# Code-row loads moved behind the last first-layer weight load, GpSimd's memsets ahead of its one-hots, and GELU's square between ScalarE's one-hots

## The chip, the core and the metric

The kernel runs on one core of one Trainium2 chip. The metric is device time in microseconds: the median over several runs, lower is better. The engines are TensorE (PE, its weight loads PEld), VectorE (DVE), ScalarE (ACT), GpSimd (POOL) and SyncE (SP), whose queue issues most DMA transfers.

## What is computed

One layer of a hybrid decoder trunk for 256 tokens of width 2048: a norm, one input projection, a pooling mixer beside a gated recurrence, an output projection, and then a product-key retrieval (PEER) over 128 x 128 single-neuron experts with 8 heads and the top 16 each. The change touches the retrieval only:

```python
q = (zc @ peer_wq).reshape(PEER_CHUNK, PEER_HEADS, 2, PEER_HALF)
s1 = einsum('chd,hkd->chk', q[:, :, 0], k1); s2 = einsum('chd,hkd->chk', q[:, :, 1], k2)
v1, i1 = top_k(s1, 16); v2, i2 = top_k(s2, 16)
...
top_s, top_pos = top_k(cand, 16)
expert = take_along_axis(cand_idx, top_pos)            # i1 * 128 + i2
gate = softmax(top_s)
act = gelu(einsum('chkd,cd->chk', take(peer_u, expert), zc))
w = gate * act
return einsum('chk,chkd->cd', w, take(peer_v, expert))
```

So each token has 128 chosen experts (8 heads x 16), each named by a pair (i1, i2) of numbers below 128.

## The kernel before

**The stages.** The front part (mixers and projections) comes first and is not touched. The *first expert layer* multiplies all 16384 rows of the first 1536 columns of `peer_u` with all tokens: 192 weight units (64 pairs of keys, GU = 3 units each) of 128 x 1024 numbers. Each unit is loaded by SP (line 99, `raw<-in_u_dram`), split into a rounded part `hi` by ACT (line 109) and a rest `lo` by DVE (line 110), and used in 24 matmuls (lines 359 to 361). ACT carries finished scores to `sw` (line 862). The other 512 columns are gathered row by row on POOL (line 684) and dotted on DVE (line 694) into `sg`. `sw` then holds every expert's score, from which the *slot stage* takes the chosen ones: 32 slots of 8 tokens. The *second expert layer* (lines 1095 to 1097) streams `peer_v` against the weights that the slot stage has written back to `sw`.

**A slot.** `extract_mm(n)` (lines 982 to 993) makes 8 small bf16 matmuls (986) of bits of i2, kept in a code buffer, with a table of codes, which push every wrong i2 far down, and adds to them the product of a one-hot of i1 (`ohts`, four buffers) with the scores (991). `extract_pick(n)` (996, DVE) takes the maximum. After every fourth slot GELU is computed for 32 tokens: `gelu_1` (DVE, 1004 and 1005), `gelu_1s` (ACT, a Square, 1009), `gelu_2` (DVE, 1013 and 1014), `gelu_2s` (ACT, a Tanh, 1018), `gelu_3` (DVE, 1022), which writes the weights `wt`. With LAG = 6 slots between, `form_mm(f)` (1063) multiplies a one-hot of i1 by a weighted one-hot of i2, and `form_out` (1067, ACT) writes the result to `sw`. `one(n)` makes the one-hot of i1: on ACT, eight Abs (1033) and a Relu (1036), or on DVE, one comparison (1029); the strings `O1_BY` and, for the last six slots, `O1_LAST` say which ("a" or "d"). `two(n)` makes the weighted one-hot of i2: on DVE a comparison (1049) and a product (1058), and on POOL (1045) the tokens that `by_pool` gives it, which in the last six slots are two of eight.

**What sets the order.** Each engine and each DMA queue runs its instructions in the order of the program, and this order is written out by hand: there is no scheduler here. In the first layer `u` counts the units; at unit `nu - 11` the work for the slot stage begins. `load_ib(k)` (869, SP) brings the i1 of slot k to all partitions (`ibt`, two buffers, 256 KB each), `onehot_t(k)` (882 on POOL or DVE, 879 and 880 on ACT) makes the transposed one-hots from them, `prepare_codes()` clears the table tile `asw` on POOL (894), copies the code table into it on ACT (897), and calls `code_tile(k)`, which clears a code buffer on POOL (906) and then loads four times 8 KB into it from SP (909). The three code buffers lie in the tiles `i1f`, `i2f` and `sg`. `Stream.ahead` issues the weight loads: each waits on SP for a free buffer, that is, for an earlier unit's `lo`.

Of the kernel before, what the change touches and what calls it, by code (L numbers as in the profile page):

```python
# [10 lines left out]
F32 = mybir.dt.float32  # L11
# [9 lines left out]
T = 256  # L21
# [20 lines left out]
SB = 32  # L42
TB = 32
LAG = 6
O1_BY, O1_LAST = "aaaad", "add"
O1_EARLY, O2_EARLY = 3, 5
O2_POOL, O2_POOL_LAST = (1, 0), 2
OHT_BY = "ppappdpapd"
NCB, V_LOAD, V_SPLIT = 3, 9, (14, 18)
# [109 lines left out]
def kernel(ctx: ExitStack, tc: tile.TileContext, x, cols, front, gates_w, keys, u1, u2, v1, v2,  # L159
                      g2row, gfrow, code, out):  # L160
    nc = tc.nc
# [3 lines left out]
    cst = ctx.enter_context(tc.tile_pool(name="cst", bufs=1))  # L165
# [5 lines left out]
    n_v = len(units) - v1.shape[0]  # L171
# [22 lines left out]
    zg = cst.tile([128, 2, D2], F32, name="zg", tag="zg")  # L194
# [18 lines left out]
    def bank(tag, bufs):  # L213
        return psA.tile([128, 512], F32, name=tag, bufs=bufs)
# [3 lines left out]
    st = Stream(nc, wst, xpool, units, SWITCH)  # L218
# [138 lines left out]
    def three(o, ah, al, bh, bl, first, last):  # L357

        nc.tensor.matmul(o, ah, bh, start=first, stop=False)  # L359
        nc.tensor.matmul(o, ah, bl, start=False, stop=False)  # L360
        nc.tensor.matmul(o, al, bh, start=False, stop=last)  # L361
# [211 lines left out]
    for c in range(4):  # L573
        acc = [bank("mm", 4) for _ in range(2)]
        for kp in range(8):
            wh, wl = st.take()
            for k2 in range(2):
                k = kp * 2 + k2
# [276 lines left out]
    def flush_evac():  # L855
        while evac:
            pi, ev = evac.popleft()
            if (pi // SB + 1) * SB * T > top[0]:
                while steps.queue or steps.plan:
                    steps.tick(10 ** 9)  # L860
                assert issued[0] - len(flying) >= GFIRST
            nc.scalar.activation(swb[:, pi // SB, :, pi % SB], ev[:, :T], AF.Copy)

    NP = T // 8
# [24 lines left out]
    ctab, code_buf = [], []  # L889

    def prepare_codes():

        tabs = asw[:, 3, :].bitcast(BF).rearrange("p (g k) -> p g k", g=4)
        nc.gpsimd.memset(tabs, 0.0)
        for g in range(4):
            gs = slice(32 * g, 32 * g + NCODE)
            nc.scalar.activation(tabs[gs, g, :], wtok[gs, 0, :], AF.Copy)
            ctab.append(tabs[:, g, :])
        code_buf.extend(t.rearrange("p a b c -> p (a b c)").bitcast(BF) for t in (i1f, i2f))
        code_buf.append(sg.rearrange("p a b -> p (a b)").bitcast(BF))  # L900
        code_tile(0)
        code_tile(1)

    def code_tile(k):
        if k < NCB:
            nc.gpsimd.memset(code_buf[k], 0.0)
        for q in range(4 * k, min(4 * k + 4, T // 4)):
            g = q % 4
            nc.sync.dma_start(code_buf[k % NCB][32 * g:32 * g + NCODE],
                              code_dram[:, q * 4:q * 4 + 4, :].rearrange("k t s -> k (t s)"))  # L910

    nu = 64 * GU
    done0 = done[0]
    for pr in range(64):
        acc = [bank("mm", 4) for _ in range(2)]
        for kg in range(GU):
            wh, wl = st.take()
            for j in range(2):
                for k in range(4):
                    kk = kg * 4 + k  # L920
                    o = (j * 4 + k) * 128
                    three(acc[j][:, :T], wh[:, o:o + 128], wl[:, o:o + 128], z2h[kk], z2l[kk], kk == 0, kk == KU - 1)
            flush_evac()
            if pr == 0 and kg == 0:
                for tag in ("zbhi", "zblo"):
                    g = zbpool.tile([128, 2, D2], F32, name="gat" + tag, tag=tag)
                    gbuf2 += [g[:, 0, :], g[:, 1, :]]
                g = gp.tile([128, 2, D2], F32, name="gatp", tag="gat")
                gbuf2 += [g[:, 0, :], g[:, 1, :]]
            u = pr * GU + kg  # L930
            side(min(256, done0 - (done0 - 256) * (u + 1) // (nu - DOT_END)) - done[0])
            if u == nu - DOT_END + 1:
                assert done[0] == 256
                ibt = zbpool.tile([128, 2, 8, 128], BF, name="ibt", tag="zbhi")
                ohts.append(zbpool.tile([128, 8, 128], F32, name="ohta", tag="zblo"))
                ohts.append(gp.tile([128, 8, 128], F32, name="ohtb", tag="gat"))
                for k in range(2):
                    load_ib(k)
                for k in range(2):
                    onehot_t(k)  # L940
                asw = cst.tile([128, 4, T], F32, name="asw", tag="zg")
                prepare_codes()
            if u == nu - 8:
                p = bank("tp", 2)
                for i in range(2):
                    nc.tensor.transpose(p[:, i * 128:(i + 1) * 128], sg[:, i, :], ident)
                nc.scalar.activation(asw[:, 1, :], p[:, :T], AF.Copy)
                code_tile(2)
            if u == nu - 3:
                for k in (2, 3):  # L950
                    load_ib(k)
            if u == nu - 1:
                early2 = [by8(v[1]) for v in list(st.raw_free)[:O1_EARLY]]
                for k in range(O1_EARLY):
                    nc.vector.tensor_tensor(early2[k], *rows(i2t, k), op=OP.is_equal)
        for j in range(2):
            evac.append((2 * pr + j, acc[j]))
# [49 lines left out]
    def gelu_1s(b):  # L1007
        a, g, c = gel[b]
        nc.scalar.activation(g, a, AF.Square, scale=math.sqrt(GELU_C))

    def gelu_2(b):
        a, g, c = gel[b]
        nc.vector.scalar_tensor_tensor(g, g, 1.0, a, op0=OP.add, op1=OP.mult)
        nc.vector.tensor_tensor(c, a, gtt[:, b * TB:(b + 1) * TB], op=OP.mult)

    def gelu_2s(b):
        g = gel[b][1]
        nc.scalar.activation(g, g, AF.Tanh, scale=GELU_S)
# [5 lines left out]
    def one(n, mid=lambda: None):  # L1024

        o = o1(n)
        if (O1_LAST[n % len(O1_LAST)] if n >= NP - LAG else O1_BY[n % len(O1_BY)]) == "d" and n >= O1_EARLY:
            mid()
            nc.vector.tensor_tensor(o, *rows(i1t, n), op=OP.is_equal)  # L1029
            return  # L1030
        for j in range(8):
            t = n * 8 + j
            nc.scalar.activation(o[:, j, :], iota, AF.Abs, scale=-1.0, bias=i1t[:, t:t + 1])  # L1033
            if j == 3:
                mid()
        nc.scalar.activation(o, o1(n, True), AF.Relu, scale=-1.0, bias=1.0)  # L1036
# [11 lines left out]
        k = 8 - by_pool(n)  # L1048
        nc.vector.tensor_tensor(o2(n)[:, :k], *rows(i2t, n, k), op=OP.is_equal)  # L1049

    def two(n, mid):

        if n >= O2_EARLY:
            two_a(n)
        mid()
        k = 8 - by_pool(n)
        o = o2(n)[:, :k]
        nc.vector.tensor_tensor(o, o, rows(wt, n, k)[1], op=OP.mult)  # L1058
# [7 lines left out]
    def form_out(n):  # L1066
        nc.scalar.activation(swb[:, :, n * 8:n * 8 + 8, :], fob.pop(n).rearrange("p t (b i) -> p b t i", i=SB), AF.Copy)  # L1067
# [36 lines left out]
    for n in range(NP + LAG + 1):  # L1104
        b, f = n // G - 1, n - LAG
        gelu = n % G == 0 and 0 <= b < T // TB
        if gelu:
            gelu_1(b)
        if n < NP:
            extract_mm(n)  # L1110
        if 0 <= f + 1 < NP:
            two_pool(f + 1)
        if n < NP:
            onehot_t(n + 4)
            load_ib(n + 6)
        if 0 <= f < NP:
            form_mm(f)
        if 0 <= f - 1 < NP:
            form_out(f - 1)
        if gelu:  # L1120
            gelu_1s(b)
        g2, g2s = ((lambda: gelu_2(b)), (lambda: gelu_2s(b))) if gelu else [lambda: None] * 2
        if 0 <= f + 1 < NP:
            two(f + 1, g2)
            if f + 1 >= O1_EARLY:
                one(f + 1, g2s)
            else:
                g2s()
        else:
            g2()  # L1130
            g2s()
        if n < NP:
            extract_pick(n)
        if O1_EARLY <= n + 2 < O2_EARLY:
            two_a(n + 2)
        if n < O1_EARLY:
            one(n)
        if n == V_LOAD:
            st.limit = len(units)
            while st.load():  # L1140
                pass
        if n in V_SPLIT:
            st.give_back()
            st.split()
            st.load()
        if gelu:
            gelu_3(b)
        if n == NP + 1:
            acc_bank()
            acc_bank()  # L1150
            w_split(0, slice(0, 128))
        if n in (NP + 3, NP + 4):
            c = n - NP - 3
            v_mm(0, c, 0, *st.hl[st.used + c][1:])
        if n % G == 1 and (b + 1) * TB % 128 == 0 and 0 <= b < T // TB:
            w_token((b + 1) * TB // 128 - 1)
# [50 lines left out]
    for pr in range(62):  # L1207
# [7 lines left out]
        if 16 <= pr < 48 and pr % 2 == 0:  # L1215
            n = (pr - 16) // 2
# [126 lines left out]
```

## Time and profile before

| | |
|---|---|
| median of 3 runs | 1650.94 us (1648.98 to 1651.82) |
| profiled execution: its own time | 1647.0 us |
| its span, first to last instruction | 1645.1 us |
| mean granted TensorE clock | 0.986 |
| busy share PE / PEld / DVE / ACT / POOL | 96% / 89% / 82% / 53% / 57% |
| HBM traffic over the span | 253 GB/s |

A row of the timeline gives start and length of an instruction (or of several alike in sequence), and in brackets how long its engine had waited just before and what ended that wait. Line numbers are those of the kernel before. PE is busy for 96% of the span, so that a stretch in which it is not, or in which its clock is granted at half, is what to look for.

### The profile page before, as it was taken

The page shows a single profiled execution, that of the slowest core. Times are in us where ns is not written, and L with a number is a line of the kernel's source. Part 1 is how long each engine was busy: PE and PEld are TensorE (multiplying, and loading weights), DVE is VectorE, ACT ScalarE, POOL GpSimd, SP SyncE. Part 2 cuts the span into 40 slices and gives each one's busy share as a digit, 9 for nine tenths or more (in the row PEclk, how much of TensorE's full clock was granted, in tenths as well). Part 3 has the DMA queues.
Part 4 walks back from the last instruction along what each step waited for, and adds up shares of the span by engine and source line. Part 5 has one row for each costly group of instructions (what it writes and reads, how often), then busy time and mean ns, then how long its engine had stood idle before and what let it go on. Part 6 is the DMA issues. An engine that isn't in the chain of part 4 may idle for free. (4 is left out here: it accounts for less than half of the span.)

```text
span 1645.1 us, 28958 instructions
## 1 busy us (share of the span) xinstructions
PE 1579.3 (96%) x10734; PEld 1461.1 (89%) x10734; DVE 1351.0 (82%) x2300; ACT 876.2 (53%) x1212; POOL 935.7 (57%) x753
## 2 busy tenths in 40 slices
PE   8899999999999999999999789989999999999996
PEld 8899888999999999999999789978888888888885
DVE  7799755899999997777777269888988898988897
ACT  6676544444444445445444358865555555555554
POOL 2476201267567766555554148856767876666662
PEclk9999999999999999999999899999999999999998
DMA  7455666578888888999998423209999999999992
GB/s 252 143 169 180 206 210 192 169 238 277 305 291 279 284 283 294 322 310 314 304 311 288 144 68 118 71 10 328 323 326 337 332 351 357 361 337 330 349 323 91
DMA packets 124974, 418.61 MB, mean 254 GB/s; under 512 B 18128, under 2 KB 20720, under 8 KB 124704
## 3 DMA queue, kind: packets, MB, share of 16 engines
q1 hardware_dynamic: 82528, 278.70, 51.4%
q0 software_dynamic: 42304, 138.06, 23.7%
q8 instruction: 84, 1.38, 0.3%
q14 instruction: 58, 0.48, 0.1%
HBM read 411.90 MB, written 4.78 MB: 253 GB/s over the span
## 5 line engine op out<-in xcount | busy, mean ns | idle before, releaser
L109 ACT ACTIVATE hi<-raw 128x1024 fp32r<-128x1024 f32 x390 | 413.0, 1059 | 479.2 <-PE mm L360 329.6
L110 DVE TENSOR_TENSOR lo<-raw,hi 128x1024 fp32r<-128x1024 f32 x390 | 500.4, 1284 | 199.1 <-ACT hi L109 196.9
L361 PE MATMUL mm<-zahi,lo 128*128 128x256 f32 x2016 | 576.0, 286 | 13.9 <-DVE lo L110 13.7
L359 PE MATMUL mm<-zahi,hi 128*128 128x256 f32 x2016 | 576.0, 286 | 10.3 <-ACT hi L109 10.3
L360 PE MATMUL mm<-zalo,hi 128*128 128x256 f32 x2016 | 573.8, 285 | 0.0
L1174 POOL DMA_INDIRECT gatv<-in_v_dram,e x256 | 335.9, 1312 | 170.2 <-DVE accg L1184 109.2
L361 PEld LDWEIGHTS mm<-zahi,lo 128*128 128x128 f32 x2016 | 389.6, 193 | 17.8 <-DVE lo L110 17.6
L359 PEld LDWEIGHTS mm<-zahi,hi 128*128 128x128 f32 x2016 | 389.9, 193 | 10.6 <-ACT hi L109 10.5
L360 PEld LDWEIGHTS mm<-zalo,hi 128*128 128x128 f32 x2016 | 390.0, 193 | 0.0
L1095 PE MATMUL acc<-hi,wht 128*128 128x512 f32 x512 | 200.8, 392 | 5.0 <-DVE sw L1230 3.2
L1097 PE MATMUL acc<-hi,wlt 128*128 128x512 f32 x512 | 200.5, 392 | 0.0
L1096 PE MATMUL acc<-lo,wht 128*128 128x512 f32 x512 | 200.4, 391 | 0.0
L1184 DVE SCALAR_TENSOR_TENSOR accg<-gatv,wtok,accg 128x512 f32<-128x512 f32 x252 | 184.2, 751 | 5.8 <-DMA gatv<-in_v_dram,e 5.6
L684 POOL DMA_INDIRECT sw<-in_u_dram,e x96 | 116.2, 1210 | 83.8 <-DVE sw L694 39.6
L1095 PEld LDWEIGHTS acc<-hi,wht 128*128 128x128 f32 x512 | 96.5, 189 | 25.9 <-DVE sw L1230 2.8
L1097 PEld LDWEIGHTS acc<-hi,wlt 128*128 128x128 f32 x512 | 96.7, 189 | 20.5 <-DVE wlt L1086 0.4
L1096 PEld LDWEIGHTS acc<-lo,wht 128*128 128x128 f32 x512 | 96.7, 189 | 20.3 <-DVE lo L110 0.4
L1095 PE MATMUL acc<-more,wht 128*128 128x512 f32 x256 | 100.1, 391 | 0.0
L1096 PE MATMUL acc<-more,wht 128*128 128x512 f32 x256 | 99.9, 390 | 0.0
L1097 PE MATMUL acc<-more,wlt 128*128 128x512 f32 x256 | 99.9, 390 | 0.0
L684 POOL DMA_INDIRECT gatzblo<-in_u_dram,e x54 | 61.6, 1140 | 47.7 <-DVE gatzblo L694 36.1
L684 POOL DMA_INDIRECT gatzbhi<-in_u_dram,e x54 | 60.9, 1129 | 45.3 <-DVE gatzbhi L694 29.1
(304 smaller groups left out, 2626.6 us busy)
## 6 DMA issues: line engine op xcount, KB each, us to landing
raw<-in_u_dram SPq DMA_DIRECT2D x192, 512.0 KB
raw<-in_v_dram SPq DMA_DIRECT2D x125, 512.0 KB
raw<-in_front_dram SPq DMA_DIRECT2D x114, 512.0 KB
sw<-in_v_dram SPq DMA_DIRECT2D x67, 512.0 KB
ibt<-i_dram SPq DMA_DIRECT2D x32, 256.0 KB
gatv<-in_v_dram,e POOLq DMA_INDIRECT x256, 5.8
xh<-in_x_dram SPq DMA_DIRECT2D x8, 256.0 KB
h_dram<-xh POOLq DMA_DIRECT2D x8, 256.0 KB, 4.7
```

What stands on the lines that cost most here:

```text
L109: nc.scalar.activation(s[1], r[1], AF.Copy)
L110: nc.vector.tensor_tensor(s[2], r[1], s[1].bitcast(F32), op=OP.subtract)
L359: nc.tensor.matmul(o, ah, bh, start=first, stop=False)
L360: nc.tensor.matmul(o, ah, bl, start=False, stop=False)
L361: nc.tensor.matmul(o, al, bh, start=False, stop=last)
L684: nc.gpsimd.indirect_dma_start(out=g, out_offset=None, in_=u2, in_offset=bass.IndirectOffsetOnAxis(ap=e32[:, i, sl:sl + 1], axis=0))
L1095: nc.tensor.matmul(banks[i * CV + c], whi[:, j, ts], vh[:, s], start=first, stop=False)
L1096: nc.tensor.matmul(banks[i * CV + c], whi[:, j, ts], vl[:, s], start=False, stop=False)
L1097: nc.tensor.matmul(banks[i * CV + c], wlo[:, j, ts], vh[:, s], start=False, stop=last)
L1174: nc.gpsimd.indirect_dma_start(out=g, out_offset=None, in_=v2, in_offset=bass.IndirectOffsetOnAxis(ap=e32[:, i, s:s + 1], axis=0))
L1184: nc.vector.scalar_tensor_tensor(a, g, wtok[:, i, s:s + 1], a, op0=OP.mult, op1=OP.add)
```

## The change

It has four edits.

1. In `prepare_codes()` the two code buffers are only cleared; their loads are issued later. The call, and with it the clearing of `asw`, moves ahead of `load_ib(0)`, `load_ib(1)` and their two one-hots.
2. At unit `nu - 8` the third code buffer is only cleared. At unit `nu - 2`, by when the program has issued the first layer's last weight load, all twelve code loads are issued, and behind them `load_ib(2)` and `load_ib(3)`, which stood at `nu - 3`.
3. In a slot with GELU, ACT's Square no longer stands ahead of the one-hot of i1 but after its fourth Abs (or, where the one-hot is DVE's, behind `form_out` as before), DVE's `gelu_2` no longer stands between the two steps of `two` but behind them, and ACT's Tanh no longer amid the Abs but behind the Relu.
4. `O1_LAST` goes from "add" to "ad". For slots 26 to 31 the one-hots of i1 are by d, a, d, d, a, d before and by a, d, a, d, a, d after: one leaves DVE for ACT, and slots 27 and 28 change places.

```diff
-O1_BY, O1_LAST = "aaaad", "add"
+O1_BY, O1_LAST = "aaaad", "ad"
...
-        code_tile(0)
-        code_tile(1)
+        for k in (0, 1):
+            nc.gpsimd.memset(code_buf[k], 0.0)
 
     def code_tile(k):
-        if k < NCB:
-            nc.gpsimd.memset(code_buf[k], 0.0)
         for q in range(4 * k, min(4 * k + 4, T // 4)):
...
                 assert done[0] == 256
+                asw = cst.tile([128, 4, T], F32, name="asw", tag="zg")
+                prepare_codes()
                 ibt = zbpool.tile([128, 2, 8, 128], BF, name="ibt", tag="zbhi")
...
                 for k in range(2):
                     onehot_t(k)
-                asw = cst.tile([128, 4, T], F32, name="asw", tag="zg")
-                prepare_codes()
...
-                code_tile(2)
-            if u == nu - 3:
+                nc.gpsimd.memset(code_buf[2], 0.0)
+            if u == nu - 2:
+                assert st.loaded == n_v
+                for k in range(NCB):
+                    code_tile(k)
                 for k in (2, 3):
                     load_ib(k)
...
-    def two(n, mid):
+    def two(n):
 
         if n >= O2_EARLY:
             two_a(n)
-        mid()
...
+        g1s = (lambda: gelu_1s(b)) if gelu else lambda: None
+        if 0 <= f + 1 < NP:
+            two(f + 1)
+        if O1_EARLY <= f + 1 < NP:
+            one(f + 1, g1s)
+        else:
+            g1s()
         if gelu:
-            gelu_1s(b)
-        g2, g2s = ((lambda: gelu_2(b)), (lambda: gelu_2s(b))) if gelu else [lambda: None] * 2
-        if 0 <= f + 1 < NP:
-            two(f + 1, g2)
-            if f + 1 >= O1_EARLY:
-                one(f + 1, g2s)
-            else:
-                g2s()
-        else:
-            g2()
-            g2s()
+            gelu_2(b)
+            gelu_2s(b)
```

**First place: POOL and SP near the end of the first layer.** POOL's instructions behind its last gathers (`ohta` and `ohtb` are one-hots 0 and 1, `asw`, `i1f`, `i2f` and `sg` the tiles that are cleared), before:

```order
L684 DMA gatzblo<-in_u_dram,e_2912 128x512 x2
L882 TENSOR_SCALAR ohta<-ibt,pidx 128x1024
L882 TENSOR_SCALAR ohtb<-ibt,pidx 128x1024
L894 MEMSET asw 128x512
L906 MEMSET i1f 128x512
L906 MEMSET i2f 128x512
L906 MEMSET sg 128x512
```

and after the change:

```order
L684 DMA gatzblo<-in_u_dram,e_2912 128x512 x2
L894 MEMSET asw 128x512
L902 MEMSET i1f 128x512
L902 MEMSET i2f 128x512
L882 TENSOR_SCALAR ohta<-ibt,pidx 128x1024
L882 TENSOR_SCALAR ohtb<-ibt,pidx 128x1024
L946 MEMSET sg 128x512
```

Three clearings moved ahead of two one-hots. On SP's queue the same stretch reads, before:

```order
L869 DMA ibt<-i_dram 128x1024 x2
L909 DMA i1f<-code_dram 8x512 x4
L909 DMA i2f<-code_dram 8x512 x4
L99 DMA raw_98<-in_u_dram 128x1024
L99 DMA raw_99<-in_u_dram 128x1024
L99 DMA raw_100<-in_u_dram 128x1024
L909 DMA sg<-code_dram 8x512 x4
L99 DMA raw_98<-in_u_dram 128x1024
L99 DMA raw_99<-in_u_dram 128x1024
L99 DMA raw_100<-in_u_dram 128x1024
L869 DMA ibt<-i_dram 128x1024 x5
```

and after the change:

```order
L869 DMA ibt<-i_dram 128x1024 x2
L99 DMA raw_98<-in_u_dram 128x1024
L99 DMA raw_99<-in_u_dram 128x1024
L99 DMA raw_100<-in_u_dram 128x1024
L99 DMA raw_98<-in_u_dram 128x1024
L99 DMA raw_99<-in_u_dram 128x1024
L99 DMA raw_100<-in_u_dram 128x1024
L907 DMA i1f<-code_dram 8x512 x4
L907 DMA i2f<-code_dram 8x512 x4
L907 DMA sg<-code_dram 8x512 x4
L869 DMA ibt<-i_dram 128x1024 x5
```

The six weight loads moved ahead of the twelve code loads; the next `ibt` loads stay behind both.

**Second place: ACT in the GELU slot n = 16**, from `form_out(9)` to `form_out(10)` (`tv` is GELU's scratch, `ott` the one-hot of i1), before:

```order
L1067 ACTIVATE sw<-fob 128x4x256
L1009 ACTIVATE tv<-tv 128x32
L1033 ACTIVATE ott<-iota,i1t 128x128 x4
L1018 ACTIVATE tv<-tv 128x32
L1033 ACTIVATE ott<-iota,i1t 128x128 x4
L1036 ACTIVATE ott<-ott 128x1024
L1067 ACTIVATE sw<-fob 128x4x256
```

and after the change:

```order
L1067 ACTIVATE sw<-fob 128x4x256
L1034 ACTIVATE ott<-iota,i1t 128x128 x4
L1010 ACTIVATE tv<-tv 128x32
L1034 ACTIVATE ott<-iota,i1t 128x128 x4
L1037 ACTIVATE ott<-ott 128x1024
L1019 ACTIVATE tv<-tv 128x32
L1067 ACTIVATE sw<-fob 128x4x256
```

The Square stands four Abs later, the Tanh four Abs and the Relu later.

**Third place: ACT at the end of the slot stage**, from `form_out(24)` on (`wht` is the first weight of the second layer, `wtok` the transposed weights), before:

```order
L1067 ACTIVATE sw<-fob 128x4x256 x2
L1009 ACTIVATE tv<-tv 128x32
L1033 ACTIVATE ott<-iota,i1t 128x128 x4
L1018 ACTIVATE tv<-tv 128x32
L1033 ACTIVATE ott<-iota,i1t 128x128 x4
L1036 ACTIVATE ott<-ott 128x1024
L1067 ACTIVATE sw<-fob 128x4x256
L1085 ACTIVATE wht<-sw 128x2x128
L1072 ACTIVATE wtok<-fob 128x128
L1067 ACTIVATE sw<-fob 128x4x256 x2
```

and after the change:

```order
L1067 ACTIVATE sw<-fob 128x4x256
L1034 ACTIVATE ott<-iota,i1t 128x128 x8
L1037 ACTIVATE ott<-ott 128x1024
L1067 ACTIVATE sw<-fob 128x4x256
L1010 ACTIVATE tv<-tv 128x32
L1019 ACTIVATE tv<-tv 128x32
L1067 ACTIVATE sw<-fob 128x4x256
L1034 ACTIVATE ott<-iota,i1t 128x128 x8
L1037 ACTIVATE ott<-ott 128x1024
L1085 ACTIVATE wht<-sw 128x2x128
L1072 ACTIVATE wtok<-fob 128x128
L1067 ACTIVATE sw<-fob 128x4x256 x2
```

The one-hot of slot 27 left ACT; those of slots 26 and 28 came, and that of slot 28 stands ahead of `wht` and `wtok`.

## Rows read from the trace of the kernel before

**Rows 1.** Busy time of PE in four stretches: the stretch in us from the span's start, its length, PE's busy time and matmul count, the granted clock, the busy share of the DMA engines and GB/s.

```profile
913.36:923.68 10.32, 0.00 (x1) 0.70 0.11 39
923.68:927.70 4.02, 3.56 (x15) 0.50 0.45 132
927.70:952.30 24.60, 24.60 (x205) 1.00 0.41 132
...
1035.70:1041.50 5.80, 5.79 (x41) 0.71 0.34 99
1041.50:1082.60 41.10, 41.10 (x402) 1.00 0.11 35
```

**Rows 2.** Who waited for whom on PE, ACT and POOL from 915 to 985 us: us in total, times, longest.

```profile
PE mm L359 <- ACT hi L109: 10.3, 1, 10.3
...
ACT asw L897 <- POOL asw L894: 12.7, 1, 12.7
...
POOL ohta L882 <- DMA ibt<-i_dram: 27.1, 3, 21.7
```

**Rows 3.** POOL's timeline near the end of the first layer.

```profile
915.05 2.86 POOL L882 TENSOR_SCALAR ohta<-ibt,pidx 128x1024 f32<-128x1024 bf16 x1 [21.67 <-DMA ibt<-i_dram]
...
920.69 0.52 POOL L894 MEMSET asw<- 128x512 bf16 x1
```

**Rows 4.** ACT's timeline over the same stretch.

```profile
907.52 1.06 ACT L109 ACTIVATE hi<-raw 128x1024 fp32r<-128x1024 f32 x1 [0.79 <-PE mm L360]
921.24 1.30 ACT L897 ACTIVATE asw<-wtok 8x128 bf16<-8x128 f32 x4 [12.66 <-POOL asw L894]
...
946.46 1.06 ACT L109 ACTIVATE hi<-raw 128x1024 fp32r<-128x1024 f32 x1 [0.78 <-PE mm L360]
...
952.74 1.11 ACT L879 ACTIVATE oht<-ibt,pidx 128x1024 f32<-128x1024 bf16 x1
```

**Rows 5.** DVE's timeline: the end of the last dot that reads `zg`, the tile in whose place `asw` is put.

```profile
904.60 0.08 DVE L694 DVE_READ_ACCUMULATOR gatzblo<-gatzblo,zg 128x1 f32 x1
```

**Rows 6.** SP's queue: its issues, several alike in one row.

```profile
910.28 0.86 SPq L869 DMA_DIRECT2D ibt<-i_dram  x2
...
937.28 3.21 SPq L99 DMA_DIRECT2D raw<-in_u_dram  x2
...
960.63 1.30 SPq L909 DMA_DIRECT2D i1f<-code_dram  x4
962.03 4.89 SPq L869 DMA_DIRECT2D ibt<-i_dram  x2
```

**Rows 7.** Two steps of the chain that ended last: start, us, what. Each is an `ibt` load from its issue to its landing.

```profile
953.88 3.22 DMA ibt<-i_dram
...
962.03 3.40 DMA ibt<-i_dram
```

**Rows 8.** ACT's timeline in the slot stage.

```profile
1016.78 0.23 ACT L1009 ACTIVATE tv<-tv 128x32 f32<-128x32 f32 x1 [0.51 <-DVE tv L1005]
...
1041.78 2.43 ACT L1033 ACTIVATE ott<-iota,i1t 128x128 f32<-128x128 f32 x8
1044.24 1.06 ACT L1036 ACTIVATE ott<-ott 128x1024 f32<-128x1024 f32 x1
1045.20 1.01 ACT L1067 ACTIVATE sw<-fob 128x1024 f32<-128x1024 f32 x1
1046.11 2.43 ACT L1033 ACTIVATE ott<-iota,i1t 128x128 f32<-128x128 f32 x8
...
1090.91 0.65 ACT L1085 ACTIVATE wht<-sw 128x256 fp32r<-128x256 f32 x1
1092.93 0.28 ACT L1072 ACTIVATE wtok<-fob 128x128 f32<-128x128 f32 x1 [1.36 <-PE fob L1071]
```

**Rows 9.** PE's timeline in the slot stage: `form_mm` of slots 14, 27, 28, 29 and 30.

```profile
1035.71 2.62 PE L1063 MATMUL fob<-ott 128*128 128x128 f32 x16 [1.94 <-DVE ott L1029]
...
1090.16 2.52 PE L1063 MATMUL fob<-oht,ott 128*128 128x128 f32 x16 [3.28 <-ACT ott L1036]
...
1093.26 2.86 PE L1063 MATMUL fob<-ott 128*128 128x128 f32 x16 [0.36 <-ACT wtok L1072]
1095.96 1.95 PE L1063 MATMUL fob<-oht,ott 128*128 128x128 f32 x16
...
1100.65 2.05 PE L1063 MATMUL fob<-ott 128*128 128x128 f32 x16 [1.37 <-ACT ott L1036]
```

**Rows 10.** DVE's timeline in the slot stage.

```profile
1030.36 1.23 DVE L110 TENSOR_TENSOR lo<-raw,hi 128x1024 fp32r<-128x1024 f32 x1 [2.15 <-ACT hi L109]
...
1055.02 0.25 DVE L1013 SCALAR_TENSOR_TENSOR tv<-tv 128x32 f32<-128x32 f32 x1 [1.95 <-ACT tv L1009]
...
1083.49 1.22 DVE L1029 TENSOR_TENSOR ott<-iota,i1t 128x1024 f32<-128x1024 f32 x1
1084.63 1.22 DVE L996 TENSOR_REDUCE asw<-exb 128x8 f32<-128x1024 f32 x1
...
1086.21 0.95 DVE L1049 TENSOR_TENSOR oht<-iota,i2t 128x768 f32<-128x768 f32 x1
```

**Rows 11.** Who PE waited for from 1107 us to the end, in the second expert layer.

```profile
PE acc L1095 <- DVE sw L1230: 3.2, 2, 2.3
PE acc L1095 <- ACT wht L1085: 1.8, 1, 1.8
```

## The prediction

> **What bounds the kernel now.** PE is the bound, so I looked first at the windows of PE for a stretch in which it does not run. There is one long one: from 913.36 to 923.68 us, near the end of the first expert layer, it has no matmul, and in the 4.02 us behind it its clock is granted at 0.50, that is 1.2 GHz in place of 2.4 [rows 1]. The table of waits names the chain: PE waits 10.3 us for ACT's `hi`, ACT waits 12.7 us for POOL's clearing of `asw`, and POOL waits up to 21.7 us for an `ibt` load [rows 2]. The timelines put them in order. POOL has nothing to do for 21.67 us until the `ibt` load has landed at 915.05, makes two one-hots, and only then clears `asw` at 920.69 [rows 3]. ACT, in whose queue the four copies into `asw` stand ahead of the next weight split, starts them at 921.24 [rows 4]. Nothing in these copies needs `ibt`: it is an order on a queue, and `zg`, in whose place `asw` lies, was last read at 904.7 [rows 5].
>
> Behind it comes the slot stage, where PE, ACT and DVE are nearly even. Undisturbed, PE needs 4.1 us for a slot (41.10 us for 402 matmuls, 40 to a slot) [rows 1]. ACT needs 4.33 us for a slot whose one-hot it makes (from Abs at 1041.78 to Abs at 1046.11) [rows 8], and so falls behind by 0.26 us in each and catches up where DVE makes it. In the second layer PE waits 5.0 us in all, and only at its two ends [rows 11]: a shift of its start goes through to the end.
>
> **The change part by part.**
>
> *The stall (edit 1).* The splits at 907.52 and 946.46 are nine units apart and stand 38.94 us from each other [rows 4]. A unit is 24 matmuls of 0.12 us each at full clock (24.60 us for 205) [rows 1], so nine units are 25.92 us; the two transposes among them, 0.24 us, stay. Lost are 38.94 - 25.92 - 0.24 = 12.8 us: the gap of 10.3, about 2.0 by the half clock (half of 4.02), and half a us of waiting for `lo`. After the change POOL can clear `asw` from 904.7 on, at 0.52 us a clearing [rows 3, 5]; ACT is through with its split at 908.58, makes the four copies in 1.30 us until 909.9, and has its next split due at 907.52 + 2.88 = 910.4 [rows 4]. They fit with 0.5 us to spare. The one-hots that POOL now makes later still wait for `ibt`, as before, and are done by 920.7 [rows 3]; the first slot needs them at about 940. So I count the whole **-12.8 us**. If the copies were 1 us late the loss would be 0.5 us; the bounds of this term are -12.8 and -12.0.
>
> *The loads (edit 2).* On SP the twelve code loads now stand behind the last weight load, and two `ibt` loads behind them. The last weight load was out at 940.5 (937.28 + 3.21) [rows 6]; it waits for a `lo`, so it moves with PE to 927.7. Four code loads take 1.30 us to issue [rows 6], twelve 3.9: until 931.6; the two `ibt` issues take 0.9 [rows 6]: until 932.5. An `ibt` load lands 3.2 to 3.4 us behind its issue [rows 7], and the first pair made POOL wait 4.8 us (910.28 to 915.05) [rows 3, 6]: landing at 935.7 to 937.3. ACT wants it at 952.74 - 12.8 = 939.9 [rows 4]. Cost: 0, with 2.6 us to spare at the least; the cover is the last four units of the first layer. The clearing of `sg` waits for transposes that also move earlier, and is far ahead of its load. No weight load is behind a code load any more, which only helps.
>
> One thing speaks against it: whether the twelve small loads run one behind the other. The `ibt` load issued at 962.03 right behind four code loads landed in 3.40 us, the one issued with none just ahead in 3.22 [rows 6, 7]: four of them cost 0.2 us, so twelve about 0.6. The Trainium skill (DMA: Bandwidth & Descriptors, Anatomy of one DMA) puts a fixed cost of about 2 us on each DMA, nearly all of it the wait for the write to be confirmed, which is latency; read as occupancy it would be an estimated 24 us here and a sum of about +3 us in place of -12.5, and the 3.40 against 3.22 us do not agree with that reading.
>
> *GELU's order (edit 3).* What it takes away: ACT's waits for `gelu_1` ahead of the Abs, 0.51 us at 1016.78 [rows 8], and DVE's wait for the Square, 1.95 us at 1055.02 [rows 10]. Only what reaches PE counts. The 0.51 us does: ACT is behind from there on, its `hi` at the split in slot 18 comes late, DVE waits 2.15 us for it [rows 10], its one-hot of slot 14 comes late, and in slot 20 PE waits 1.94 us [rows 9] and then runs at a clock of 0.71 on average for 5.80 us, where a slot at full clock takes 4.1 [rows 1]: 1.7 more. With 0.5 us less of waiting this wait is 1.4 us; the gain is 0.5 if the clock still falls and 2.2 if it does not (PE's 1.37 us of waiting at 1100.65 was followed by a `form_mm` of 2.05 us, not 2.62) [rows 9]. I take 0.7, near the lower end, because DVE's later `gelu_2` and `gelu_3` in slots 12 and 16 (below) eat into the 0.5. The 1.95 us of DVE does not count: PE runs without a gap from 1041.5 to 1082.6 [rows 1].
>
> What it adds: DVE's `gelu_2` now waits for a Square behind four Abs (half of the 2.43 us for eight, about 1.2) [rows 8] and `gelu_3` for a Tanh behind the Relu (another 1.2 + 1.0). Queued behind them on DVE are `extract_pick` and the next slot's `two`; POOL's part of `two` waits for `wt` as well. With LAG = 6, `form_mm` of the slots concerned comes two slots (8.2 us) later. DVE's own room is smaller: I put 0 to 2 us on this for the stage and take 0.3.
>
> *The last slots (edit 4).* I follow the queues in the time of the rows. The one-hot of slot 26 leaves DVE, so the pick at 1084.63 moves up by 1.14 to 1083.49. Behind it: 1.58 us for the pick and `gelu_1` (1084.63 to 1086.21), two steps of `two` at 0.9 each, the one-hot of 27 now on DVE at 1.2 [rows 10], so that it is out at about 1088.1: `form_mm(27)` starts at 1088.2 and not at 1090.16 [rows 9], 1.9 earlier. But ACT then has, behind the Tanh at about 1088.6, `form_out` 0.9, the one-hot of 28 (2.47 + 0.96), `wht` 0.6 and `wtok` 0.3 [rows 8], ending at 1093.8, and `form_mm(28)` waits for `wtok`: 0.5 later than its 1093.26 [rows 9]. DVE's `wlt` waits for the same `wht`, with the one-hot of 29 behind it: `form_mm(29)` at about 1097 in place of 1095.96 [rows 9]; ACT's one-hot for `form_mm(30)` is out at 1100.4 to 1101 in place of 1100.6. The stage ends between 0.7 us earlier and 0.4 later; and PE has again a wait of some 3.5 us ahead of `form_mm(28)`, so a second fall of the clock can add 1.7 to 2. Bounds -0.7 and +2.4; I take **+0.7**.
>
> The sum: -12.8 + 0 - 0.7 + 0.3 + 0.7 = -12.5 us. Against the profiled execution's 1647.0 us this is 1634.5. That execution lies 3.9 us below the median of the three runs; against the median, 1650.94, it is 1638.4 us. I forecast the median.
>
> **The rivals.**
>
> *More than the stall.* The clock does not fall in slot 20 (-2.2) and the last slots come out well (-0.7): -12.8 - 2.2 - 0.7 = -15.7, 1635.2 us. For it speaks the 1.37 us wait that left the clock alone, against it that 1.4 is the middle of an estimate. 12%.
>
> *Slower: the code loads hold up the slot stage.* If twelve small loads took their landing time one behind the other, with 3.2 us each as for an `ibt` load [rows 7], they would need 38 us from 927.7, and the two `ibt` loads would land at 969 where ACT wants them at 939.9: +29 - 12.5 = +16.5, 1667 us. It decides from 2.6 us of delay on, and the result is slower than before from 15 us on, 1.3 us a load. Against it stand the 0.2 us for four. 2%; a partial delay of 3 to 8 us, 1641 to 1646, another 3%.
>
> *GELU's waits reach PE.* In the five GELU slots with an ACT one-hot (slots 8, 12, 16, 20 and 28) DVE waits up to 2.2 us longer, and each time PE stops and its clock falls (1.7): up to 19.5 us in all and +7 us, 1658 us. It decides from the point where DVE has less than that in hand against PE. Against it: PE has no gap from 1041.5 to 1082.6 although DVE was late by 1.95 there [rows 1, 10]. 1%; half of it or less, 1641 to 1648, 3%.
>
> *The change does not do what it says:* ACT's copies wait for something else than POOL's place in the queue, and the stall stays, 1651 to 1653 us. The clearing has no other producer than the dots that end at 904.7 [rows 5]. 2%.
>
> **How the numbers follow.** The forecast, 1638.4 us, has 77%, the rival with more 12%, the others 11% together. The bounds of edits 1, 3 and 4 reach from -15.7 to, with all the bad ends together, -12.0 - 0.5 + 2 + 2.4 = -8.1: 1635.2 to 1642.8. On either side I add about 1 us for the spread of the medians (the three runs of before lie within 2.8 us): 1633.5 to 1643.5. Outside lie the cases in which loads or GELU take more. About 0.2%, 3.3 us, is what a measurement of this kernel can tell from no change. Faster by more than that (under 1647.6): 94%; within it: 3%; slower: 3%.
>
> **What would show it.** In the profile of the changed kernel: POOL's clearing of `asw` at about 905 us, ACT's copies at 908.6 without a wait, no gap in PE from 905 to 939.5 and a clock of 1.00 there; the first `exb` matmul right behind, at about 940; ACT's `oht` at 939.9 without a wait for `ibt`; PE's wait ahead of `form_mm(27)` shorter than 3.28 us and the one ahead of `form_mm(28)` longer than 0.36. Wrong would be a wait for `ibt` or a code load at 940, a gap that only moved, or more than four waits of PE over 1.5 us in the slot stage.

## The result, and the profile after

| | median, us | runs |
|---|---|---|
| before | 1650.94 | 7 (1648.12 to 1652.96) |
| after | 1642.40 | 7 (1636.94 to 1645.17) |

The ratio of after to before is 0.995, with a 95% interval of 0.9933 to 0.9966: 0.5% or 8.5 us less, clear of the noise, where 12.5 us were forecast. The median lies 4.0 us above the forecast and inside the range. The profiled execution of after took 1645.17 us, with a span of 1643.3, only 1.8 less than the span before; why so little is the first thing to explain.

PE near the end of the first layer and at the end of the slot stage of after (columns as in [rows 1]):

```profile
905.00:939.37 34.37, 34.37 (x289) 1.00 0.59 184
...
1080.00:1110.00 30.00, 23.96 (x129) 0.83 0.16 50
```

The gap of 10.32 us and the half clock behind it [rows 1] are gone: 34.37 us without a pause, at full clock. But from 1080 to 1110 the clock is granted at 0.83. POOL's timeline of after, against [rows 3]:

```profile
910.47 0.52 POOL L894 MEMSET asw<- 128x512 bf16 x1 [11.98 <-DVE gatzblo L694]
...
920.27 3.77 POOL L882 TENSOR_SCALAR ohta<-ibt,pidx 128x1024 f32<-128x1024 bf16 x1 [8.36 <-DMA ibt<-i_dram]
```

And ACT's, against [rows 4]:

```profile
913.24 1.06 ACT L109 ACTIVATE hi<-raw 128x1024 fp32r<-128x1024 f32 x1 [0.79 <-PE mm L360]
914.20 1.28 ACT L897 ACTIVATE asw<-wtok 8x128 bf16<-8x128 f32 x4
...
939.37 1.06 ACT L109 ACTIVATE hi<-raw 128x1024 fp32r<-128x1024 f32 x1 [0.77 <-PE mm L360]
...
945.64 1.11 ACT L879 ACTIVATE oht<-ibt,pidx 128x1024 f32<-128x1024 bf16 x1
```

The clearing no longer waits for an `ibt` load but for the last dot, the copies follow the split at once, and the splits nine units apart stand 26.13 us from each other, not 38.94. SP's queue, against [rows 6]:

```profile
918.46 14.94 SPq L99 DMA_DIRECT2D raw<-in_u_dram  x6
933.71 1.35 SPq L907 DMA_DIRECT2D i1f<-code_dram  x4
935.10 1.89 SPq L907 DMA_DIRECT2D i2f<-code_dram  x4
937.10 1.28 SPq L907 DMA_DIRECT2D sg<-code_dram  x4
938.42 15.15 SPq L869 DMA_DIRECT2D ibt<-i_dram  x5
```

The twelve code loads take 4.7 us to issue, and ACT's one-hot at 945.64 waits for nothing.

To see where the rest went I cut every profiled span at four places that all kernels have: ACT's split ahead of the `asw` copies; the first `exb` matmul (always 6.53 us behind the layer's last split); the first matmul of slot 8; the first `acc` matmul behind the second `wht` (1107.65 in the profile before). All in us; the table holds the experiments too.

| kernel, profile | to the split | split to first `exb` | to slot 8 | slot 8 to `acc` | `acc` to the end | median of runs |
|---|---|---|---|---|---|---|
| before, 1st | 907.52 | 45.47 | 29.21 | 125.45 | 537.45 | 1650.94 |
| before, 2nd (r_before_a) | 917.72 | 45.08 | 27.21 | 125.41 | 536.08 | |
| before, 3rd (r_before_b) | 916.20 | 45.40 | 26.65 | 125.74 | 537.11 | |
| after | 913.24 | 32.66 | 29.14 | 128.39 | 539.87 | 1642.40 |
| after (r_after) | 912.99 | 32.65 | 29.15 | 128.18 | 538.03 | 1642.41 |
| e_memsets: edit 1 | 914.61 | 34.24 | 27.53 | 125.37 | 540.05 | 1641.36 |
| r_memsets: edit 1 | 913.71 | 33.93 | 27.52 | 125.31 | 536.93 | 1639.99 |
| e_loads_memsets: 1, 2 | 915.60 | 32.66 | 26.73 | 125.40 | 537.21 | 1638.36 |
| e_no_last: 1, 2, 3 | 913.01 | 32.66 | 29.03 | 127.31 | 539.09 | 1639.21 |
| e_no_gelu: 1, 2, 4 | 911.32 | 32.67 | 29.08 | 123.91 | 536.82 | 1637.23 |
| r_no_gelu: 1, 2, 4 | 912.01 | 32.67 | 29.28 | 123.97 | 537.17 | 1637.08 |
| x_old_at_d | 914.84 | 32.67 | 29.04 | 123.91 | 537.64 | 1640.01 |
| r_old_at_d | 913.43 | 32.66 | 29.35 | 123.89 | 539.37 | 1639.39 |
| x_tail | 913.11 | 32.65 | 29.28 | 124.14 | 535.42 | 1637.29 |

Read down the columns. The second and the fourth go with the kernel to within 0.4 us; the others differ between executions of kernels that hold the same program there. In the first profile of before the first piece, the same program in all rows, was 4 to 10 us shorter than in any other, so the two spans shown first differ by far less than the medians. The mean of the two profiles of after against that of the three of before: -0.7 up to the split, -12.7 from there to the first `exb`, +1.5 to slot 8, +2.8 from there to `acc`, +2.1 behind it.

### The profile page after: what moved, and what is told of

It reads as the page before. It is cut to its first block, busy times and chain, and to the rows that moved or that the text cites. A ratio compares the mean times of both kernels' runs of the same rounds, so it can differ in the third digit from the quotient of the medians.

```text
span 1643.3 us, 28965 instructions
## 1 busy us (share of the span) xinstructions
PE 1580.7 (96%) x10734; PEld 1458.5 (89%) x10734; DVE 1353.4 (82%) x2299; ACT 879.4 (54%) x1221; POOL 934.8 (57%) x753
## 4 chain that ended last, share of the span: by engine, by line
PE 76%; DVE 9%; ACT 6%; DMA 6%; issue 2%; POOL 1%; another core or an unknown queue 0%; SPq 0%; ACTq 0%; DVEq 0%; POOLq 0%
PE mm L361 14%; PE mm L360 14%; PE mm L359 14%; PE acc L1096 8%; PE acc L1097 8%; PE acc L1095 8%; DMA raw<-in_v_dram 3%; DVE lo L110 3%; PE mm L585 2%; PE mm L584 2%; ACT hi L109 2%; PE mm L583 2%; ACT ott L1034 2%; PE fob L1063 1%; DMA raw<-in_u_dram 1%
## 5 line engine op out<-in xcount | busy, mean ns | idle before, releaser
L361 PE MATMUL mm<-zahi,lo 128*128 128x256 f32 x2016 | 574.5, 285 | 18.2 <-DVE lo L110 18.2
L684 POOL DMA_INDIRECT sw<-in_u_dram,e x96 | 112.0, 1166 | 94.5 <-DVE sw L694 45.9
```

Of the source, the lines that this page charges most:

```text
L684: nc.gpsimd.indirect_dma_start(out=g, out_offset=None, in_=u2, in_offset=bass.IndirectOffsetOnAxis(ap=e32[:, i, sl:sl + 1], axis=0))
```

## The experiments

After the result my theory was that the slot stage lost what the forecast lacks, through edit 3; the rivals were edit 4, and chance. Letters of theories are those of the texts on record; the first four runs, on one chip, have their own. On that chip before had a median of 1651.53 us.

**Edits 1 and 2 alone** (after, with GELU's lines and `O1_LAST` as before):

```diff
-O1_BY, O1_LAST = "aaaad", "ad"
+O1_BY, O1_LAST = "aaaad", "add"
```

> Edits 1 and 2 alone (memsets first on POOL, code loads behind the last weight load); GELU's order and O1_LAST as before. Theory A (the stall is worth 12.8 us and edits 3 and 4 together lengthen the slot stage by about 2.9 us, as the one profile of the change shows): the slot stage, from the first exb matmul to the first acc matmul behind the second wht, takes 154.7 us as before, and the time is 1638 us, 3 to 5 below the change. Theory B (edits 3 and 4 cost nothing, and the slot stage is longer because of the moved loads or by chance): the slot stage takes about 157.5 us here too, or the time is that of the change, 1642 us.

Measured: 1638.36 us (1635.83 to 1640.06), ratio 0.9912 (0.9896 to 0.9927). Two of the four edits give more than all four. The slot stage took 152.1 us, less than either theory said, because its piece up to slot 8 was 2.5 us shorter than in the first profile of before; from slot 8 on it is as before (125.40), as theory A has it.

**Without edit 4** (the same line of the diff alone).

> The change with O1_LAST as before (edits 1, 2 and 3). Theory A1 (the lengthening is edit 4's, at the last slots): PE's wait ahead of form_mm(28) is again about 0.4 us, the slot stage takes 153 to 155 us, the time is about 1638 us. Theory A2 (it is edit 3's, GELU's order in the middle slots): the slot stage takes 157 us or more, 1642 us.

Measured: 1639.21 us (1634.86 to 1643.02), ratio 0.9911 (0.9894 to 0.9929). From slot 8 on it takes 127.31 us, 1.9 more than with the old order of GELU and the old last slots: edit 3 costs something by itself. The whole stage, 156.3 us, lies between the two theories; PE's wait ahead of `form_mm(28)` was 0.79 us. Of the 1.9 us, 0.8 lie between slots 8 and 31 and 1.1 behind slot 31. The one-hot of slot 32 is ACT's in this kernel, so that the second part is not the wait that is found below for a DVE one-hot; where it comes from is not shown.

**Without edit 3** (GELU's lines as before, the rest as after).

> The change with GELU's old order (edits 1, 2 and 4). Theory A1 (the lengthening is edit 4's): the wait of about 1.9 us ahead of form_mm(28) stays, the slot stage takes 156 to 158 us, 1641 us. Theory A2 (edit 3's): the slot stage takes 154 to 155 us, 1638 us.

Measured: 1637.23 us (1634.03 to 1641.83), ratio 0.9912 (0.9892 to 0.9931). From slot 8 on 123.91 us: edit 4 without edit 3 gains 1.5 (against 125.40 with edits 1 and 2 alone), edit 3 on top of it costs 4.4. The whole stage, 153.0 us, is shorter than either theory said, on the side of A2.

**Edit 1 alone** (before, with `asw` and `prepare_codes()` moved up; the code loads stay at their old places).

> Edit 1 alone: the memsets and table copies ahead of load_ib(0), load_ib(1) and their one-hots on POOL, with code_tile(0) and (1) loading right there and everything else as before. Theory A (the order on POOL alone made the stall): no gap in PE near the end of the first layer, the split before the table copies and the first layer's last split 26.1 us apart in place of 38.9, 1638 us, the same as edits 1 and 2 together. Rival (the code loads on SP ahead of the weight loads were a part of it): a gap of 1 us or more stays, 1640 us or more.

Measured: 1641.36 us (1636.07 to 1645.15), ratio 0.9926 (0.9906 to 0.9946). From the split to the first `exb` it takes 34.24 us, 1.58 more than with edit 2, and PE waits there for `hi` and `lo`, 0.3 and 0.8 us: as the rival has it, though most of the gap is gone.

**That kernel once more**, on another chip (before there: 1651.37 us).

> Edit 1 alone, once more: the clearing of asw goes first, the code loads stay in their old places ahead of the weight loads. If these loads hold up the weight loads behind them: 27.2 to 28.2 us from the split ahead of the asw copies to the last one of the layer (26.13 with edit 2), with ACT's waits for raw in 920 to 940 us adding to over 2 us, and a median of 1639 to 1642. If the 1.58 us were chance: 26.1 to 26.6 us, and a median of 1637 to 1639.

Measured: 1639.99 us (1637.60 to 1645.06), ratio 0.9938 (0.9918 to 0.9959), and 27.40 us from split to last split. SP's queue in that run:

```profile
916.69 1.35 SPq L909 DMA_DIRECT2D i1f<-code_dram  x4
918.09 1.87 SPq L909 DMA_DIRECT2D i2f<-code_dram  x4
920.06 0.82 SPq L869 DMA_DIRECT2D ibt<-i_dram  x2
920.99 4.03 SPq L99 DMA_DIRECT2D raw<-in_u_dram  x3
930.64 1.30 SPq L909 DMA_DIRECT2D sg<-code_dram  x4
932.06 2.98 SPq L99 DMA_DIRECT2D raw<-in_u_dram  x3
```

and ACT's timeline:

```profile
926.76 1.06 ACT L109 ACTIVATE hi<-raw 128x1024 fp32r<-128x1024 f32 x1 [0.81 <-DMA raw<-in_u_dram]
...
935.92 1.06 ACT L109 ACTIVATE hi<-raw 128x1024 fp32r<-128x1024 f32 x1 [2.49 <-DMA raw<-in_u_dram]
```

The weight loads from 920.99 on stand behind eight code loads, those from 932.06 on behind four more, and ACT's splits wait 3.3 us for weights; with edit 2 no split there does. The longer of the two waits, 2.49 us, is for the first weight load of the second group. The four code loads ahead of that group were held up on SP for 5.5 us by POOL's clearing of `sg`, which this run makes at 930.10, behind the two one-hots: a wait on a queue once more, and not only the time of small loads. So edit 2 is worth 1.3 to 1.6 us in this piece, shown twice.

**The changed kernel and the one without edit 3 once more**, as partners on a third chip (before there: 1650.06 us).

> The changed kernel once more, as a partner for the next three. Theory S (slot 24): its new order of GELU costs time in the slots whose one-hot is DVE's, 24 and 32, where ACT's Tanh waits over 2.5 us for a gelu_2 that stands behind that one-hot on DVE; so again 25.4 us from slot 25 to slot 31, 28 to 30 us from slot 31 to the first acc matmul, and a median 2.5 to 5 us above the same kernel with the old order of GELU. Rival R (the waits for the Square): the cost sits in the slots whose one-hot is ACT's; the same numbers here. Rival N (chance): the two orders are the same within 0.2%, and the 3 to 4 us between the profiles were falls of the clock that come and go.

Measured: 1642.41 us (1638.86 to 1645.20), ratio 0.9947 (0.9932 to 0.9962). From slot 31 to `acc` it took 29.4 us, as expected, but from slot 25 to slot 31 24.8 and not 25.4: 0.5 us of the loss lay ahead of slot 25 this time. From slot 8 to slot 31 the two profiles of this kernel agree, 98.8 us.

> The changed kernel with GELU in the old order (edits 1, 2 and 4), once more, beside the changed kernel. Theories S and R: 1636 to 1638.5 us, 0.15 to 0.3% under the changed kernel; 24.4 us from slot 25 to slot 31, about 26 from slot 31 to the first acc matmul. Rival N: within 0.1% of the changed kernel.

Measured: 1637.08 us (1636.65 to 1639.82), ratio 0.9925 (0.9912 to 0.9939), 0.32% under its partner, a little more than expected. Chance (rival N) is out for the stage: 128.4 and 128.2 us against 123.9 and 124.0.

**The old order of GELU in slots 24 and 32 alone**, where the one-hot of i1 is DVE's:

```diff
+        if gelu and n in (24, 32):
+            gelu_1s(b)
+            two(f + 1, lambda: gelu_2(b))
+            one(f + 1, lambda: gelu_2s(b))
+        else:
```

> The changed kernel, but GELU in the old order in slots 24 and 32 alone, the two whose one-hot is DVE's; the new order stays where ACT makes the one-hot (8, 12, 16, 20, 28). Theory S: the Tanh of slot 24 waits under 0.5 us, 24.4 to 24.7 us from slot 25 to slot 31, 26 to 27 from slot 31 to the first acc matmul, and a median of 1636 to 1639 us, within 0.1% of the old order everywhere. Rival R: 25.4 and 28 to 30 us as in the changed kernel, and its median.

Measured: 1640.01 us (1637.10 to 1641.56), ratio 0.9935 (0.9920 to 0.9949). From slot 8 on 123.91 us: the whole 4.4 us are gone, as theory S has it, and rival R (the other five slots) is refuted for this kernel. From slot 25 to 31 it took 24.55 us and from slot 31 to `acc` 25.94, where 24.4 to 24.7 and 26 to 27 were expected. The rows show the mechanism. ACT in slot 24 of after:

```profile
1047.31 0.22 ACT L1010 ACTIVATE tv<-tv 128x32 f32<-128x32 f32 x1
1050.15 0.23 ACT L1019 ACTIVATE tv<-tv 128x32 f32<-128x32 f32 x1 [2.62 <-DVE tv L1014]
1050.29 1.00 ACT L1067 ACTIVATE sw<-fob 128x1024 f32<-128x1024 f32 x1
1051.19 2.44 ACT L1034 ACTIVATE ott<-iota,i1t 128x128 f32<-128x128 f32 x8
```

DVE in the same slot:

```profile
1046.82 1.22 DVE L1058 TENSOR_TENSOR oht<-oht,asw 128x1024 f32<-128x1024 f32 x1
1047.96 1.22 DVE L1030 TENSOR_TENSOR ott<-iota,i1t 128x1024 f32<-128x1024 f32 x1
1049.09 1.02 DVE L1014 SCALAR_TENSOR_TENSOR tv<-tv 128x32 f32<-128x32 f32 x1
```

And ACT in slot 24 with the old order there:

```profile
1048.83 0.22 ACT L1010 ACTIVATE tv<-tv 128x32 f32<-128x32 f32 x1
1049.81 0.23 ACT L1019 ACTIVATE tv<-tv 128x32 f32<-128x32 f32 x1 [0.75 <-DVE tv L1014]
1050.17 1.02 ACT L1068 ACTIVATE sw<-fob 128x1024 f32<-128x1024 f32 x1
1051.09 2.43 ACT L1034 ACTIVATE ott<-iota,i1t 128x128 f32<-128x128 f32 x8
```

ACT's Square is out at 1047.5, but `gelu_2` (1014) now stands behind the product of `two` and the one-hot on DVE, 2.3 us of work. The Tanh waits 2.62 us for it, and with it `form_out` and the next one-hot, which stand behind it on ACT and need nothing from GELU. With the old order the wait is 0.75 (under 0.5 was expected). Its median was 2.9 us above that of r_no_gelu where 0.1% was expected; theory S does not explain that, and a second run was made.

> The changed kernel with GELU in the old order in slots 24 and 32 alone, once more. Its slot stage was as short as with the old order everywhere (152.95 us against 152.99 and 153.25), but its median 2.9 us longer. Theory S with chance for the rest: slot stage 152.9 to 153.4 again, the median 1636.5 to 1640, at 0.991 to 0.9935 of the kernel before. Rival R2 (the new order in the other slots costs time elsewhere): at 0.9935 or more again, with the excess in the same segment, ahead of the slot stage.

Measured: 1639.39 us (1632.81 to 1641.72), ratio 0.9922 (0.9900 to 0.9945), 123.89 us from slot 8 on. As expected with chance, but the medians of both runs lie 2 to 3 us above those of the kernel without edit 3, in pieces that hold the same program: whether that is chance stays open. What the two slots cost is shown in the stage, and only in part in the medians.

**The last one-hots dealt otherwise** (without edit 3):

```diff
-O1_BY, O1_LAST = "aaaad", "ad"
+O1_BY, O1_LAST = "aaaad", "adaddd"
```

> Edits 1 and 2, the old order of GELU, and the last one-hots dealt otherwise: slot 26 ACT, 27 DVE, 28 DVE, 29 DVE, 30 ACT, 31 DVE (the changed kernel: ACT and DVE in turn). If ACT sets the end of the stage (it is late by 0.25 us in each slot whose one-hot it makes, and wtok stands behind its queue), one more one-hot on DVE shortens slot 31 to the first acc matmul from 25.9 to 25.0 to 25.5 us: 1 us under the kernel with the old order. If DVE sets it, 26 to 27.5 us, and 0 to 1.5 us above.

Measured: 1637.29 us (1635.95 to 1642.31), ratio 0.9926 (0.9912 to 0.9941); 26.16 us from slot 31 to `acc` against 25.93. Relieving ACT brings nothing: DVE is as late.

**Two more profiles of before.**

> The kernel before, for a second profile. In its first profile ACT's split ahead of the copies into asw began at 907.52 us; in eight profiles of kernels that are word for word the same up to there it began at 911.3 to 915.6. Theory C (chance): the start of this split varies from execution to execution with the waits for the weight loads, whatever the kernel; here 909 to 916 us, in line with a whole time of 1649 to 1653. Rival K (kernel): the edits behind that place make the part ahead of it longer; here 906.5 to 908.5 again. Both: from that split to the last one of the layer 38.9 us.

> The kernel before, for a third profile. Theory C: the split at 909 to 916 us, and not at the same time as in the second profile. Rival K: 906.5 to 908.5.

Measured: 1653.44 and 1652.88 us, the split at 917.72 and 916.20. Later than either theory said, but the same kernel's executions lie 10 us apart there: that is no effect of the edits, and rival K is refuted. What is left is chance (theory C), or the chip, which these runs do not tell apart.

## Why the prediction was right, and where not

The median lies in the range because edits 1 and 2 together gave what the sum has for the stall, which is nearly the whole sum. For edits 3 and 4 together the sum has +0.3 us and the stage gave +2.8; that this is not more is luck, since a cost of 4.4 us that the sum lacks was set off in part by a gain of 1.5 that it did not forecast either. The range held it because its upper end adds up all the bad ends. (Its lower end lies 1.7 us beyond the bounds and its upper one 0.7, not 1 us each.)

- **The stall (-12.8).** Right in place and mechanism, and in size for edits 1 and 2 together: from the split to the first `exb` 45.08 to 45.47 us became 32.66, -12.4 to -12.8. Edit 1 by itself, to which the whole term was given, falls short of its bounds (next point). The clearing ran as soon as the dots were done, and the half us to spare for the copies was enough.
- **The loads (0).** No delay came, but the term was mis-sized: edit 1 alone gives -11.2 (34.1 on average for 45.3), and edit 2 the other -1.4, because the weight loads are no longer behind the code loads and their wait for POOL. "Only helps" should have had a price. The `ibt` load issued right behind the twelve small loads, at 938.42, was there before 945.64. The Trainium skill (DMA: Bandwidth & Descriptors, Anatomy of one DMA) gives about 2 us for each DMA, for those that GpSimd issues, and calls it mostly latency; these loads are SP's. Read as occupancy, 2 us a load would have held this load back until an estimated 24 us behind 933.71. The trace does not agree with that reading, only with one of latency.
- **GELU's order (-0.7 + 0.3): the step that failed.** ACT no longer waits 0.51 us ahead of the Abs [rows 8], but in slot 16 of after it waits 0.20 for the Square and 0.91 for the Tanh, whose `gelu_2` is now behind DVE's product:

```profile
1010.48 0.23 ACT L1010 ACTIVATE tv<-tv 128x32 f32<-128x32 f32 x1 [0.20 <-DVE tv L1006]
...
1013.87 0.23 ACT L1019 ACTIVATE tv<-tv 128x32 f32<-128x32 f32 x1 [0.91 <-DVE tv L1014]
```

  PE's wait ahead of `form_mm(14)` was 1.97 us (1.94 before), so the gain of 0.7 did not come; and the part of it that was to come from the clock could not. The half clock behind this wait, which I had priced at 1.7 us, comes in some executions only, and slots 20 to 24 take the same time with it as without it. Two profiles with the old order, first e_no_gelu and then r_memsets, from the first matmul of slot 20 to that of slot 25 (us, then busy time of PE, PEld, DVE, ACT and POOL, clock, DMA share, GB/s):

```profile
1022.05:1046.60 24.55, 21.65 (x203) 20.68 (x201) 22.32 (x28) 18.93 (x45) 21.07 (x8) 1.00 0.30 87
1024.15:1048.70 24.55, 22.64 (x202) 22.11 (x200) 22.32 (x28) 18.93 (x45) 21.07 (x8) 0.93 0.29 86
```

  With the clock at full PE waits 0.99 us more, for ACT's one-hot, ahead of `form_mm(15)`. The profiled execution of after has no half clock there either, so the condition of the rival with -15.7 came in it, and its 2.2 us did not.

  For the new waits I had looked at the five slots with an ACT one-hot, where DVE waits for ACT. In sum they cost nothing: x_old_at_d and r_old_at_d, which keep the new order there, take 98.0 us from slot 8 to slot 31 like the two profiles without edit 3, and after and r_after take 98.8. The cost lies in the two slots that I left out, 24 and 32, and in the other direction, ACT waiting for DVE: 0.8 us ahead of slot 31 and 3.5 to 3.6 behind it, 4.2 to 4.5 us together, twice the upper bound of 2.
- **The last slots (+0.7).** In the two profiles of after, slot 31 to `acc` took 29.6 and 29.4 us against 27.3 to 27.4, +2.1, within the bounds, and with the falls of the clock that I had named as the bad end. But this is edit 3 at work. The chain that ended last in after (start, us, what):

```profile
1081.46 1.22 DVE ott L1030
1082.68 0.11 DVE tv L1014
...
1082.81 0.23 ACT tv L1019
1083.04 0.91 ACT sw L1067
1083.95 2.34 ACT ott L1034 x8
...
1087.28 0.62 ACT wht L1085
1087.90 0.17 ACT wtok L1072
...
1088.11 2.08 PE fob L1063 x8
```

  DVE's one-hot of slot 27, then `gelu_2`, then the Tanh (it had waited 2.87 us), `form_out`, the one-hot of 28, `wht` and `wtok`, and only then PE. With the old order in slot 32 this Tanh comes 6.4 us behind slot 31's start (1080.93 in x_old_at_d) and not 9.0, and edit 4 alone *shortens* the end, to 25.9 us: -1.4, outside my bounds. I had put the Tanh at 8.3 (1088.6), too late for edit 4 alone. PE in r_no_gelu:

```profile
1080.41 2.02 PE L1064 MATMUL fob<-oht,ott 128*128 128x128 f32 x16 [1.40 <-DVE asw L1023]
...
1084.24 2.05 PE L1064 MATMUL fob<-ott 128*128 128x128 f32 x16 [1.69 <-ACT wtok L1073]
1087.79 2.02 PE L1064 MATMUL fob<-oht,ott 128*128 128x128 f32 x16 [1.50 <-DVE ott L1030]
```

  PE's five waits there add to 7.09 us (0.72, 1.40, 1.69, 1.50, 1.78), before to 7.07 (0.28, 3.28, 0.36, 1.37, 1.78). Not less waiting, but no wait of 3.28 us and so no slow `form_mm` behind it (2.52 and 2.86 in [rows 9], 2.02 to 2.05 here).
- **The rest.** +1.5 us from the first `exb` to slot 8 and +2.1 behind `acc` were in no term. The first goes with a stretch of half clock near slot 6. Eleven profiles have one (mean granted clock of the piece 0.88 to 0.94) and take 27.5 to 29.4 us; three have none (1.00: e_loads_memsets, r_before_a and r_before_b) and take 26.7 to 27.2. All eight profiles with edit 3 or 4 have it, and three of the six others; edit 3 changes nothing ahead of slot 8 and edit 4 nothing ahead of slot 26, so I have no mechanism, and whether this is more than chance stays open. The second scatters by 4.6 us among kernels that hold the same program there.
- **The rivals.** None of them came with its time. "GELU's waits reach PE" had the right edit, but not the slots and not the waiting engine. And one sign of being wrong was badly set: after has six waits of PE over 1.5 us in the slot stage, more than the four that I allowed, but before already has five, and the kernel without edit 3 has six.

The lowest medians are those of the change without edit 3: 1637.08 and 1637.23 us, with ratios of 0.9925 and 0.9912 against 0.9947 and 0.995 for the change as made. Its medians alone do not tell it from edits 1 and 2 (0.9912) or from x_tail (0.9926); against the first its stage from slot 8 on is 1.4 to 1.5 us shorter.

## What to carry to other kernels

When a step is moved on two engines that hand it back and forth, walk every place where it stands, also the slots in which another engine makes the one-hot, and write down for each wait what stands behind the waiting instruction that does not need it. A short instruction that another engine waits for belongs ahead of long ones that nobody waits for yet. Before a fall of the clock is priced, look at whether TensorE sets the pace there: where another engine does, the slow matmuls only fill a wait. And compare profiles piece by piece: here one span of before was 6 us off its two others, more than half of the whole effect.

## What was not expected of the hardware

Whether the clock falls behind a wait of one length varies between executions. In after, `form_mm(27)`:

```profile
1082.83 3.13 PE L1063 MATMUL fob<-oht,ott 128*128 128x128 f32 x16 [1.97 <-DVE tv L1014]
```

and in r_after:

```profile
1082.54 2.02 PE L1063 MATMUL fob<-oht,ott 128*128 128x128 f32 x16 [1.96 <-DVE tv L1014]
```

After 1.97 us of waiting it took 3.13 us at a mean granted clock of 0.61, after 1.96 us 2.02 at 1.00. The 1.1 us did not reach the end, since PE then waits that much less for `wtok` (1.94 us in after, 3.16 in r_after). In slot 6 such a fall did lengthen its piece. e_loads_memsets, and below it x_old_at_d, the same program up to there, with waits of 1.96 and 1.90 us ahead of the slot's first matmul:

```profile
965.32 2.00 PE L992 MATMUL exb<-sw,oht 128*128 128x128 f32 x16
969.06 2.02 PE L1064 MATMUL fob<-raw,hi 128*128 128x128 f32 x16 [1.73 <-DVE raw L1059]
```

```profile
964.48 2.88 PE L992 MATMUL exb<-sw,oht 128*128 128x128 f32 x16
969.14 3.49 PE L1064 MATMUL fob<-raw,hi 128*128 128x128 f32 x16 [1.78 <-DVE raw L1059]
```

The piece from the first `exb` to slot 8 took 26.73 us in the one and 29.04 in the other.

The other surprise is the spread of one and the same stretch, 907.5 to 917.7 us to the split. PE's waits for `lo` in it add to 13.3 us in the first profile of before and to 15.8 to 18.2 in the other thirteen; that is up to half of the spread, and the rest was not followed up.
